# The MLP's down projection as seven products of half blocks, with the weights' sums made by accumulating DMAs

## The chip, the core and the metric

The kernel runs on one core of one Trainium2 chip, in one launch. A core has a matrix engine (TensorE, PE in the profile, with PEld for its weight loads), a vector engine (VectorE, DVE), a scalar engine (ScalarE, ACT), a general one (GpSimd, POOL), an engine that only issues DMAs (SyncE, SP), and 16 DMA engines. Each engine has a queue of its own and works it off in order; semaphores connect them. The metric is the device time of one execution in microseconds, the median of several runs.

## The reference

Two groups of 256 tokens go through one encoder layer with shared weights. The change concerns only its end, the MLP, where `x` has 512 rows (both groups), 1024 columns, and the hidden layer has 4096:

```python
h2 = rms_norm(x, norm2_g)
x = x + jnp.square(jax.nn.relu(h2 @ w_up)) @ w_down
...
return rms_norm(x, final_norm_g)
```

All of it is fp32. The norm's factor per token is taken out of the up projection: `relu(r*z)**2` is `r**2 * relu(z)**2`, so the factor is applied when the down projection's result is added.

## The kernel before

**Precision.** An fp32 product is made of three matmuls with operands in a faster format: each operand is split into a high part (ACT copies it with rounding) and a low part (DVE, in the attention part POOL, subtracts the high part from the original). `mm3` issues high x high, high x low, low x high. A "split" below means such a pair of instructions, "hi" and "lo" its two results.

**Weights.** A weight chunk is 128 x 1024 (512 KB). `chunk` has SP load it into one of two `raw` tiles and splits it into two of ten `w` tiles. `run` walks a list of units, each a function with the chunks that it needs; after a unit has been issued, the chunks of the next ones are fetched, three chunks ahead in the MLP (`ahead`), four in its last quarter. So in the queues of ACT and DVE the split of a chunk stands three units ahead of the unit that uses it. ACT, DVE and PE keep the order in which the program was written (`InOrder`); the DMAs of SP and GpSimd's instructions are placed by the framework, by when their tiles come free.

**The MLP.** `up` makes one tile of 128 hidden units for all 512 tokens: 24 matmuls of 128 x 512 (8 blocks of the inner dimension by three), then `r` = relu (ACT), its square (DVE), and the split of the square into `u` (ACT and DVE). There are four quarters of eight such tiles. After each quarter the down projection uses its eight tiles: for each half `hh` of the 1024 output columns and each block `t` of 128 tokens, 24 matmuls into one PSUM bank, then one DVE instruction (`add_down`) that adds the bank, times the token's factor `rr`, into `acc[t, hh]` in SBUF. Those start out as `x` turned back to rows of tokens (`turn_x1`, four PE transposes, a copy and a square on ACT).

**The end.** The last half of the last quarter is `last_down`: tokens block by block, so that the final norm of one block (`final`: a sum, a power on GpSimd, scaling on ACT and DVE, two DMAs out) runs beside the matmuls of the next.

Of the kernel before, what the change touches and what calls it, by code (L numbers as in the profile page):

```python
# [10 lines left out]
F32 = mybir.dt.float32  # L11
# [5 lines left out]
P = 128  # L17
# [60 lines left out]
def encoder_kernel(ctx: ExitStack, tc: tile.TileContext, a: dict, out: bass.AP):  # L78
# [4 lines left out]
    sb = ctx.enter_context(tc.tile_pool(name="sb", bufs=1))  # L83
    ps = ctx.enter_context(tc.tile_pool(name="ps", bufs=8, space=bass.MemoryType.PSUM))
    dr = ctx.enter_context(tc.tile_pool(name="dr", bufs=1, space=bass.MemoryType.DRAM))

    cnt = [0]

# [79 lines left out]
    def run():  # L168
        need = [(i, s) for i, (_, srcs) in enumerate(units) for s in srcs]
        got, at = [[] for _ in units], 0  # L170
        done = 0
        for i, (fn, srcs) in enumerate(units):
            done += len(srcs)
            for fetch in (True, False):
                while at < min(len(need), done + (0 if fetch else ahead[0])):
                    u, s = need[at]
                    got[u].append(chunk(*s))
                    at += 1
                if fetch:
                    fn(*got[i])  # L180

    def mm3(o, wh, wl, xh, xl, first, last):
        E.matmul(o, wh, xh, start=first, stop=False)
        E.matmul(o, wh, xl, start=False, stop=False)
        E.matmul(o, wl, xh, start=False, stop=last)

    def fm(w, X, o):

# [515 lines left out]
    def put_v12(t, p):  # L704

        b, i = divmod(t, 2)
        for rl in range(2):
            v = sb.tile([P, S], F32, tag="v12", name=nm("v12"), bufs=8)
# [105 lines left out]
        unit(out_proj, (a["w_o"][ff],))  # L814


    acc = {}
    ss = const("ss", [P, NT, 2])
    rr = const("rr", [P, NT])

    def turn_x1(t, hh):
# [25 lines left out]

    gf = []
    fs = const("fs", [P, NT, 3])
    fr = const("fr", [P, NT])  # L850

    def load_gf():
        for hh in range(2):
            g = wide("gf")
            A.dma_start(g, bass.AP(tensor=a["gf"].tensor, offset=a["gf"].offset + hh * T, ap=[[0, P], [1, T]]))
            gf.append(g)

    def add_down(t, hh, p, last=False):
        y = acc[t, hh]
        V.scalar_tensor_tensor(y, p, rr[:, t:t + 1], y, op0=ALU.mult, op1=ALU.add)  # L860
        if last:
            A.activation(wide("junk"), y, AF.Square, accum_out=fs[:, t, 0:1])
            V.tensor_tensor(y, y, gf[hh], op=ALU.mult)

    def final(t, c, n):

        r = fr[:, t:t + 1]
        V.tensor_reduce(r, fs[:, t, :n], axis=AX.X, op=ALU.add)
        V.tensor_scalar(r, r, 1.0 / D, EPS, op0=ALU.mult, op1=ALU.add)
        G.tensor_tensor(r, r, mhalf[:, 0:1], op=ALU.pow)  # L870
        V.tensor_tensor(acc[t, 1][:, c], acc[t, 1][:, c], gf[1][:, c], op=ALU.mult)
        A.activation(acc[t, 0], acc[t, 0], AF.Copy, scale=r)
        V.tensor_scalar(acc[t, 1], acc[t, 1], r, None, op0=ALU.mult)
        for hh in range(2):
            (A, SP)[hh].dma_start(out[t * P:(t + 1) * P, hh * 512:(hh + 1) * 512], acc[t, hh])

    def last_down(*ws):

        flush(NT)
        Uq = U[3]  # L880
        for t in range(NT):
            c = slice(t * P, (t + 1) * P)
            cols = ((0, 512),) if t < NT - 1 else ((0, 256), (256, 512))
            for part, (n0, n1) in enumerate(cols):
                p = bank()[:, :n1 - n0]
                for k in range(KD):
                    wh, wl = ws[k // 2]
                    w = slice((k % 2) * 512 + n0, (k % 2) * 512 + n1)
                    mm3(p, Uq[k][:, 0, c], Uq[k][:, 1, c], wh[:, w], wl[:, w], k == 0, k == KD - 1)
                y = acc[t, 1][:, n0:n1]  # L890
                V.scalar_tensor_tensor(y, p, rr[:, t:t + 1], y, op0=ALU.mult, op1=ALU.add)
                A.activation(wide("junk")[:, n0:n1], y, AF.Square, accum_out=fs[:, t, 1 + part:2 + part])
                if n1 < 512:
                    V.tensor_tensor(y, y, gf[1][:, n0:n1], op=ALU.mult)
            final(t, slice(n0, n1), 1 + len(cols))

    for qq in range(4):
        for ff in range(KD):
            unit(lambda w, qq=qq, ff=ff: up(w, qq, ff), (a["w_up"][8 * qq + ff],))
            if qq == 0:  # L900
                unit(lambda ff=ff: turn_x1(ff // 2, ff % 2))
        if qq == 0:
            unit(inv_ms)
            unit(load_gf)
        uq = U.setdefault(qq, [])
        if qq == 3:
            unit(lambda: ahead.__setitem__(0, 4))
        for hh in range(2):
            srcs = [a["w_dn"][qq, hh, i] for i in range(4)]
            if qq == 3 and hh:  # L910
                unit(last_down, *[(s,) for s in srcs])
            else:
                def after(t, p, hh=hh, qq=qq):
                    if qq < 3:
                        add_down(t, hh, p)
                    else:
                        later.append(lambda: add_down(t, hh, p, True))

                for u in tm(uq, srcs, 512, after):
                    unit(*u)  # L920
    run()


# [72 lines left out]
```

## Time and profile before

| what | us |
|---|---|
| median of 3 runs (871.85 to 873.25) | 871.92 |
| the profiled execution, its own time | 871.41 |
| its span, first to last instruction | 869.6 |
| PE busy in it | 858.7 |
| DVE busy | 390.1 |
| ACT busy | 344.7 |
| POOL busy | 192.6 |
| DMA: mean rate over the span | 101 GB/s |

The page's first part gives the busy time of each engine; the second cuts the span into 40 slices with the busy tenths; the fourth follows the chain of work that ended last; the fifth groups instructions by line and operation. Most instructions have line 72, since a helper records them, so groups are told by their tiles' names. In an answer of the timeline a row is: start, duration, engine, line, operation, output<-inputs, shape, count, and in brackets how long the engine had been idle and what ended that. A duration there reaches a little into the next row, since an engine starts an instruction before the one ahead has quite finished.

### The profile page before, as it was taken

The page shows a single profiled execution, that of the slowest core. Times are in us where ns is not written, and L with a number is a line of the kernel's source. Part 1 is how long each engine was busy: PE and PEld are TensorE (multiplying, and loading weights), DVE is VectorE, ACT ScalarE, POOL GpSimd, SP SyncE. Part 2 cuts the span into 40 slices and gives each one's busy share as a digit, 9 for nine tenths or more (in the row PEclk, how much of TensorE's full clock was granted, in tenths as well). Part 3 has the DMA queues.
Part 4 walks back from the last instruction along what each step waited for, and adds up shares of the span by engine and source line. Part 5 has one row for each costly group of instructions (what it writes and reads, how often), then busy time and mean ns, then how long its engine had stood idle before and what let it go on. Part 6 is the DMA issues. An engine that isn't in the chain of part 4 may idle for free.

```text
span 869.6 us, 10683 instructions
## 1 busy us (share of the span) xinstructions
PE 858.7 (99%) x4176; PEld 717.3 (82%) x4176; DVE 390.1 (45%) x625; ACT 344.7 (40%) x606; POOL 192.6 (22%) x133
## 2 busy tenths in 40 slices
PE   9999999999999999999999999999999999999997
PEld 8778998888888888888887888888888888888886
DVE  6595445456443213333436444433453345334543
ACT  6364555565654332232224335521342144214432
POOL 2315455547556551112212000000000000000001
PEclk9999999999999999999999999999999999999999
DMA  8342223233332122222323432332223222322222
GB/s 284 113 136 88 83 73 103 80 93 98 106 94 71 51 87 96 96 86 97 121 73 99 149 117 96 122 119 74 95 98 121 74 95 98 123 73 93 97 77 98
DMA packets 41851, 88.00 MB, mean 101 GB/s; under 512 B 18734, under 2 KB 18980, under 8 KB 41800
## 3 DMA queue, kind: packets, MB, share of 16 engines
q1 hardware_dynamic: 39272, 83.07, 29.3%
q10 hardware_dynamic: 2304, 4.20, 1.5%
q8 instruction: 33, 0.54, 0.3%
q14 instruction: 18, 0.15, 0.1%
q0 software_dynamic: 224, 0.05, 0.0%
HBM read 85.15 MB, written 2.14 MB: 100 GB/s over the span
## 4 chain that ended last, share of the span: by engine, by line
PE 88%; DVE 4%; ACT 2%; DMA 2%; issue 2%; POOL 1%; SPq 0%; POOLq 0%; DVEq 0%; ACTq 0%
PE ps L72 81%; PE sc L72 3%; PE o L72 2%; PE tp L72 2%; DMA mr<-in_memT 1%; DMA raw<-in_w_mem 1%; ACT sp L72 1%; DVE sp L72 1%; DVE w L72 1%; DVE mg L72 0%; ACT w L72 0%; DVE st L72 0%; DVE qq L72 0%; DVE kl L72 0%; DVE sq L72 0%
## 5 line engine op out<-in xcount | busy, mean ns | idle before, releaser
L72 PE MATMUL ps<-x,w 128*128 128x512 f32 x1080 | 252.4, 391 | 0.0
L72 PEld LDWEIGHTS ps<-x,w 128*128 128x128 f32 x1080 | 200.8, 188 | 41.5
L72 DVE TENSOR_TENSOR w<-raw,w 128x1024 fp32r<-128x1024 f32 (+1 forms) x107 | 131.3, 1234 | 128.7 <-ACT w L72 128.6
L72 ACT ACTIVATE w<-raw 128x1024 fp32r<-128x1024 f32 (+2 forms) x144 | 149.1, 1040 | 95.4 <-DMA raw<-in_w_dn 37.4
L72 PE MATMUL ps<-h,w 128*128 128x512 f32 x768 | 176.7, 390 | 0.0
L72 PE MATMUL ps<-w,u 128*128 128x512 f32 (+1 forms) x792 | 175.1, 383 | 0.0
L72 PEld LDWEIGHTS ps<-w,u 128*128 128x128 f32 x792 | 145.5, 188 | 29.0
L72 PEld LDWEIGHTS ps<-h,w 128*128 128x128 f32 x768 | 143.6, 188 | 29.6
L158 POOL TENSOR_TENSOR w<-raw,w 128x1024 fp32r<-128x1024 f32 (+1 forms) x37 | 87.3, 2361 | 117.8 <-ACT w L72 95.0
L870 POOL TENSOR_TENSOR fr<-fr,mhalf 128x1 f32<-128x1 f32 x4 | 3.5, 870 | 395.9 <-DVE fr L72 395.9
L72 ACT ACTIVATE r<-ps 128x512 f32<-128x512 f32 x32 | 19.1, 598 | 114.4 <-PE ps L72 114.4
L72 DVE TENSOR_TENSOR r<-r 128x512 f32<-128x512 f32 x32 | 22.1, 692 | 70.8 <-ACT r L72 70.8
L72 ACT ACTIVATE sp<-sp,st 128x256 f32<-128x256 f32 (+1 forms) x48 | 25.8, 538 | 57.7 <-DVE st L72 57.7
L72 DVE SCALAR_TENSOR_TENSOR acc<-ps,rr,acc 128x512 f32<-128x512 f32 (+1 forms) x33 | 24.2, 733 | 54.3 <-PE ps L72 54.3
L72 PE MATMUL ps<-mg,w 128*128 128x512 f32 x192 | 44.3, 390 | 1.5 <-ACT mg L72 0.9
L72 ACT ACTIVATE g<-ps 128x512 f32<-128x512 f32 x16 | 9.6, 598 | 91.0 <-PE ps L72 91.0
L72 PEld LDWEIGHTS ps<-mg,w 128*128 128x128 f32 x192 | 36.0, 188 | 9.6 <-ACT mg L72 1.3
L72 PE MATMUL ps<-w,x 128*128 128x384 f32 (+1 forms) x192 | 39.9, 363 | 0.0
L72 DVE TENSOR_TENSOR sum<-o,lo 64x256 f32<-64x256 f32 x24 | 10.0, 418 | 66.5 <-ACT lo L72 66.4
L457 POOL TENSOR_TENSOR sp<-sp,st 128x512 f32<-128x512 f32 (+1 forms) x32 | 36.7, 1147 | 6.5 <-DVE st L72 3.6
L72 PEld LDWEIGHTS ps<-w,x 128*128 128x128 f32 x192 | 34.3, 188 | 3.6
L72 DVE TENSOR_TENSOR u<-r,u 128x512 fp32r<-128x512 f32 x32 | 22.2, 692 | 22.4 <-ACT u L72 22.4
(135 smaller groups left out, 814.4 us busy)
## 6 DMA issues: line engine op xcount, KB each, us to landing
raw<-in_w_up SPq DMA_DIRECT2D x32, 512.0 KB, 3.2
raw<-in_w_dn SPq DMA_DIRECT2D x32, 512.0 KB, 3.3
raw<-in_w_g SPq DMA_DIRECT2D x24, 512.0 KB, 3.3
raw<-in_w_b SPq DMA_DIRECT2D x12, 512.0 KB, 3.2
raw<-in_w_bam SPq DMA_DIRECT2D x8, 512.0 KB, 3.2
raw<-in_w_o SPq DMA_DIRECT2D x8, 512.0 KB, 3.3
raw<-in_w_mem SPq DMA_DIRECT2D x7, 512.0 KB, 4.3
bias<-scr SPq DMA_DIRECT2D x48, 64.0 KB, 3.0
```

The source lines that it names most:

```text
L72: return self.tc.keep_in_program_order(method(*args, **kw))
L158: sub[0].tensor_tensor(lo[:, c], raw[:, c], f(hi[:, c]), op=ALU.subtract)
L457: G.tensor_tensor(s[:, :, :w], s[:, :, :w], st[:, 6:8].unsqueeze(2).to_broadcast([P, 2, w]), op=ALU.mult)
L870: G.tensor_tensor(r, r, mhalf[:, 0:1], op=ALU.pow)
```

## The change

The down projection's inner dimension is now taken in eight pieces `c` of 512 (four tiles of `up`). Within a piece both matrices are cut into 2 x 2 halves: A11, A12, A21, A22 (tokens by hidden units, 256 x 256) and B11, B12, B21, B22 (hidden units by output columns, 256 x 512). Instead of eight products of halves, seven are made of sums and differences of halves (`product`), each of 12 matmuls of 128 x 512 for two blocks of 128 tokens, in four pairs of PSUM banks, a, c, d and e. P1 and P2 share bank a, Q5 and Q3 bank d, P7 and Q4 bank e: the second adds onto what the first has left there, after DVE has read the first.

What the seven products need and leave:

- the weights' halves and their sums. A piece has four `blk` tiles (`load_blocks`, SP's DMAs). The tile T is B11 at first; after each split DVE and ACT are through with it, and a DMA issued by GpSimd with `accum_op=ALU.add` adds the next half from DRAM onto it: P1 uses B11, Q5 the sum with B12, Q6 that with B22, Q4 that with B21. C is B12 with B22 added in the same way.
- the sums of A (`form`): up to one DVE subtraction each, then a split (ACT copy, DVE subtraction).
- the sums of the products (`add_to`): each bank is added by DVE into one of five accumulators (V, G, 11, 12, 21; two tiles each), the first time copied by ACT. The final combination with the residual is made once, in the last piece (`last_sums`).

`up` now takes the square on ACT, in fp32, without a split. The units are put in turn: in a piece, a product of the piece before stands between two tiles of `up`, four of the seven so, and three more follow without a tile of `up` between them. After the last tile of `up` ten products are left: P7, Q3, Q4 of piece 6 and all seven of piece 7, the latter in the order P1, Q5, P2, Q6, P7, Q3, Q4. The residual goes to DRAM (`x1d`) and comes back before the last piece. The pools of the attention (`at`) are closed before the MLP so that `blk` has room.

The diff, cut to its core:

```diff
+    def load_blocks(c):
+
+        if c in blocks:
+            return
+        t = {n: block_tile() for n in "T2BC"}
+        for n, b in (("T", "11"), ("2", "21"), ("C", "12"), ("B", "22")):
+            SP.dma_start(t[n], block(c, b))
+        G.dma_start(t["C"], block(c, "22"), accum_op=ALU.add)
+        blocks[c] = t
+
+    def parts(c, n):
+
+        def go():
+            load_blocks(c)
+            hi, lo = w_tile(), w_tile()
+            src = blocks[c][n[0]]
+            A.activation(hi, src, AF.Copy)
+            V.tensor_tensor(lo, src, f(hi), op=ALU.subtract)
+            if n[1:]:
+                G.dma_start(src, block(c, n[1:]), accum_op=ALU.add)
+            return hi, lo
+        return go
...
+    PRODUCTS = dict(P1=("T12", "a", "V", -1), P2=("2", "a", "11", 1), Q5=("T22", "d", "G", 1),
+                    Q6=("T21", "c", "V", 1), P7=("C", "e", "G", -1), Q3=("B", "d", "12", 1), Q4=("T", "e", "21", 1))
+
+    def product(w, c, name):
+        _, bk, to, sign = PRODUCTS[name]
+        x = forms.pop((c, name))
+        new = name in ("P1", "Q5", "Q6", "P7")
+        for i in range(2):
+            if new:
+                banks[bk, i] = bank()
+            p = banks[bk, i]
+            for j in range(2):
+                t = slice(j * S + i * P, j * S + (i + 1) * P)
+                k = slice(j * 512, (j + 1) * 512)
+                mm3(p, x[:, 0, t], x[:, 1, t], w[0][:, k], w[1][:, k], new and j == 0, j == 1, not new)
+        flush(9)
+        ps_ = [banks[bk, i] for i in range(2)]
+        if c < NC - 1:
+            later.append(lambda: [add_to(to, i, ps_[i], ALU.add if sign > 0 else ALU.subtract) for i in range(2)])
+        else:
+            later.append(lambda: last_sums(name, ps_))
...
+            elif name == "Q6":
+                add_to("V", i, p)
+                for k in ("12", "G"):
+                    V.tensor_tensor(acc[k, i], acc[k, i], acc["V", i], op=ALU.add)
+                V.tensor_tensor(acc["21", i], acc["21", i], acc["V", i], op=ALU.subtract)
+                scaled(y[lo, 1], lo, 1, acc["12", i])
+                scaled(y[hi, 1], hi, 1, acc["G", i])
+                scaled(y[hi, 0], hi, 0, acc["21", i])
+            elif name == "P7":
+                finish(hi, 1, y[hi, 1], p, -1)
+            elif name == "Q3":
+                finish(lo, 1, y[lo, 1], p)
+                final(lo)
...
+    def finish(t, hh, y, p, sign=1):
+        scaled(y, t, hh, p, sign)
+        A.activation(h2("junk"), y, AF.Square, accum_out=fs[:, t, hh:hh + 1])
+        V.tensor_tensor(y, y, gf[0][:, hh], op=ALU.mult)
...
+    for c in range(NC):
+        for m in range(4):
+            if c:
+                down(c - 1, m)
+                make(c - 1, m + 3)
+            unit(lambda w, ff=4 * c + m: up(w, ff), (a["w_up"][4 * c + m],))
+            if c == 0:
+                unit(lambda m=m: turn_x1(m, 0))
+                unit(lambda m=m: turn_x1(m, 1))
...
+        for n in range(3):
+            if c:
+                down(c - 1, 4 + n)
+            make(c, n)
+    unit(fetch_x1)
+    for n in range(7):
+        down(NC - 1, n)
+        if n < 4:
+            make(NC - 1, n + 3)
+    unit(lambda: flush(9))
```

Three places show how the queues stand now. The first is ACT between the first MLP tiles and the first down product. Before, around the fourth tile of `up` (r is the relu, u the hi of the square, w a chunk's hi, acc and junk the transposed residual):

```order
L72 ACTIVATE r_4530<-ps_4505 128x512
L72 ACTIVATE u_4533<-r_4530 128x512
L72 ACTIVATE w_4537<-raw_4536 128x1024
L72 ACTIVATE acc_4547<-tp_4542 128x512
L72 ACTIVATE junk_4549,ss<-tp_4542 128x512
L72 ACTIVATE r_4576<-ps_4551 128x512
```

Now, from the relu of the fourth tile to the hi of P1's form (f_4604):

```order
L72 ACTIVATE r_4573<-ps_4548 128x512
L72 ACTIVATE u_4493<-r_4573 128x512
L72 ACTIVATE w_4576<-blk_4432 128x1024
L72 ACTIVATE xt_4585<-tp_4580 128x512
L72 ACTIVATE junk_4587,ss<-tp_4580 128x512
L72 DMA x1d<-xt_4585 128x512
L72 ACTIVATE xt_4595<-tp_4590 128x512
L72 ACTIVATE junk_4597,ss<-tp_4590 128x512
L72 DMA x1d<-xt_4595 128x512
L72 ACTIVATE f_4604<-u_4376 128x512
```

Where the next tile's matmuls followed, a product follows that needs f_4604, at the end of ten ACT rows.

The second place is ACT after the last tile of `up`. Before, chunk after chunk was split, each from a tile of its own:

```order
L72 ACTIVATE r_6386<-ps_6361 128x512
L72 ACTIVATE u_6389<-r_6386 128x512
L72 ACTIVATE w_6393<-raw_6392 128x1024
L72 ACTIVATE w_6399<-raw_6398 128x1024
L72 ACTIVATE w_6433<-raw_6432 128x1024
```

Now, from that tile's relu on (w_6742 is for Q4 of piece 6; w_6760, w_6782, w_6806 and w_6839 for P1, Q5, P2 and Q6 of piece 7; f are forms):

```order
L72 ACTIVATE r_6739<-ps_6712 128x512
L72 ACTIVATE u_6656<-r_6739 128x512
L72 ACTIVATE w_6742<-blk_6251 128x1024
L72 ACTIVATE w_6760<-blk_6564 128x1024
L72 ACTIVATE f_6765<-u_6528 128x512
L72 ACTIVATE w_6782<-blk_6564 128x1024
L72 ACTIVATE f_6789<-f_6787 128x512
L72 ACTIVATE w_6806<-blk_6565 128x1024
L72 ACTIVATE f_6810<-u_6656 128x512
L72 ACTIVATE w_6839<-blk_6564 128x1024
```

Three of the splits read the same tile, blk_6564 (T of piece 7): between each two of them lies an accumulating DMA that waits for the split ahead.

The third place is the end of DVE's queue. Before, four rows stood behind each of the last banks of matmuls (here the last block but one of tokens; fr is the norm's factor):

```order
L72 SCALAR_TENSOR_TENSOR acc_4639<-ps_6616,rr,acc_4639 128x512
L72 TENSOR_REDUCE fr<-fs 128x1
L72 TENSOR_SCALAR fr<-fr 128x1
L72 TENSOR_TENSOR acc_4639<-acc_4639,gf_4740 128x512
L72 TENSOR_SCALAR acc_4639<-acc_4639,fr 128x512
```

Now, from within the sums that follow Q6 (ps_6906 is its second bank) to P7's results (ps_6928 and ps_6935, the pair e, onto which Q4's matmuls add next):

```order
L72 SCALAR_TENSOR_TENSOR xt_6817<-acc_4798,rr,xt_6817 128x512
L72 SCALAR_TENSOR_TENSOR xt_6817<-acc_4948,rr,xt_6817 128x512
L72 TENSOR_TENSOR acc_4668<-acc_4668,ps_6906 128x512
L72 TENSOR_TENSOR acc_4923<-acc_4923,acc_4668 128x512
L72 TENSOR_TENSOR acc_4800<-acc_4800,acc_4668 128x512
L72 TENSOR_TENSOR acc_4950<-acc_4950,acc_4668 128x512
L72 SCALAR_TENSOR_TENSOR xt_6815<-acc_4923,rr,xt_6815 128x512
L72 SCALAR_TENSOR_TENSOR xt_6819<-acc_4800,rr,xt_6819 128x512
L72 SCALAR_TENSOR_TENSOR xt_6819<-acc_4950,rr,xt_6819 128x512
L72 SCALAR_TENSOR_TENSOR xt_6817<-ps_6928,nr,xt_6817 128x512
L72 TENSOR_TENSOR xt_6817<-xt_6817,gf_6821 128x512
L72 SCALAR_TENSOR_TENSOR xt_6819<-ps_6935,nr,xt_6819 128x512
```

Fourteen rows of sums stand between the forms of the last products and the row that frees P7's bank; behind them come the same five rows as before, four times.

More of the change, by code (lines that the diff above doesn't have):

```diff
@@ L176, in run @@
                     u, s = need[at]
-                    got[u].append(chunk(*s))
+                    got[u].append(s[0]() if callable(s[0]) else chunk(*s))
                     at += 1
@@ L180, in run, with mm3 @@
                     fn(*got[i])
[L182 to L185, printed above, removed]
+    def mm3(o, wh, wl, xh, xl, first, last, more=False):
+        E.matmul(o, wh, xh, start=first, stop=False, skip_group_check=more)
+        E.matmul(o, wh, xl, start=False, stop=False, skip_group_check=more)
+        E.matmul(o, wl, xh, start=False, stop=last, skip_group_check=more)
     def fm(w, X, o):
@@ L848, in encoder_kernel @@
[L848 to L863, printed above, removed]
@@ new lines, in encoder_kernel, with add_to @@
+    acc, banks = {}, {}
+    def add_to(k, i, p, op=ALU.add):
+        if (k, i) in acc:
+            V.tensor_tensor(acc[k, i], acc[k, i], p, op=op)
+        else:
+            acc[k, i] = h2("acc")
+            A.activation(acc[k, i], p, AF.Copy, scale=1.0 if op == ALU.add else -1.0)
+    PRODUCTS = dict(P1=("T12", "a", "V", -1), P2=("2", "a", "11", 1), Q5=("T22", "d", "G", 1),
+                    Q6=("T21", "c", "V", 1), P7=("C", "e", "G", -1), Q3=("B", "d", "12", 1), Q4=("T", "e", "21", 1))
@@ new lines, in encoder_kernel, with fetch_x1, scaled @@
+    xt, gf = {}, []
+    def fetch_x1():
+        for t in range(NT):
+            xt[t] = sb.tile([P, 2, 512], F32, tag="s4", name=nm("xt"), bufs=21)
+            SP.dma_start(xt[t], x1d[t].rearrange("p (h n) -> p h n", h=2))
+        g = sb.tile([P, 2, 512], F32, tag="s4", name=nm("gf"), bufs=21)
+        SP.dma_start(g, bass.AP(tensor=a["gf"].tensor, offset=a["gf"].offset, ap=[[0, P], [T, 2], [1, T]]))
+        gf.append(g)
+    def scaled(y, t, hh, src, sign=1):
+        V.scalar_tensor_tensor(y, src, (rr if sign > 0 else nr)[:, t:t + 1], y, op0=ALU.mult, op1=ALU.add)
@@ new lines, in last_sums @@
+    def last_sums(name, ps_):
+        for i in range(2):
+            p, lo, hi = ps_[i], i, i + 2
+            y = {(t, hh): xt[t][:, hh] for t in (lo, hi) for hh in range(2)}
+            if name == "P1":
+                add_to("V", i, p, ALU.subtract)
+            elif name == "Q5":
+                add_to("G", i, p)
+                scaled(y[lo, 0], lo, 0, acc["11", i])
+            elif name == "P2":
+                finish(lo, 0, y[lo, 0], p)
+            elif name == "Q6":
+                add_to("V", i, p)
[5 more added lines that the diff above has]
+                scaled(y[hi, 0], hi, 0, acc["21", i])
+            elif name == "P7":
+                finish(hi, 1, y[hi, 1], p, -1)
+            elif name == "Q3":
+                finish(lo, 1, y[lo, 1], p)
+                final(lo)
+            else:
+                finish(hi, 0, y[hi, 0], p)
+                final(hi)
@@ L872, in final @@
-        A.activation(acc[t, 0], acc[t, 0], AF.Copy, scale=r)
-        V.tensor_scalar(acc[t, 1], acc[t, 1], r, None, op0=ALU.mult)
+        A.activation(xt[t][:, 0], xt[t][:, 0], AF.Copy, scale=r)
+        V.tensor_scalar(xt[t][:, 1], xt[t][:, 1], r, None, op0=ALU.mult)
         for hh in range(2):
[L875 to L902, printed above, removed]
-            unit(inv_ms)
[L904 to L920, printed above, removed]
+            (A, SP)[hh].dma_start(out[t * P:(t + 1) * P, hh * 512:(hh + 1) * 512], xt[t][:, hh])
```

87 lines of the change are left out of this document (68 added, 19 removed).

## The prediction, made before the changed kernel ran

> **What bounds the kernel now.** First the page's engine table, then the chain of waits over the MLP, then the groups.
>
> ```profile
> span 869.6 us, 10683 instructions
> PE 858.7 (99%) x4176; PEld 717.3 (82%) x4176; DVE 390.1 (45%) x625; ACT 344.7 (40%) x606; POOL 192.6 (22%) x133
> 557.90 0.44 PE tp L72 x4
> 558.33 299.24 PE ps L72 x1320
> ```
>
> PE is busy 99% of the span, and from 558.33 on the chain is one run of 1320 matmuls: 299.24 / 1320 = 0.2267 us each. Nothing else ends last there, so a matmul less is worth 0.2267 us as long as PE stays fed. DVE has 55% to spare over the whole, which says nothing about one stretch.
>
> ```profile
> 863.34 0.48 DVE L72 SCALAR_TENSOR_TENSOR acc<-ps,rr,acc 128x256 f32<-128x256 f32 x1 [0.72 <-PE ps L72]
> 865.52 0.48 DVE L72 TENSOR_SCALAR acc<-acc,fr 128x512 f32<-128x512 f32 x1 [0.44 <-POOL fr L870]
> ```
>
> At the end PE is through at about 863.3; DVE's last row ends at 866.0, and the last DMA closes the span 3.6 us later. So 6.3 us lie behind PE now.
>
> **The change, part by part.**
>
> *Matmuls.* The down projection had 768 full-width matmuls (some as two halves); now 8 x 7 x 12 = 672. 96 x 0.2267 = **21.8 us** less on PE. This is the whole gain.
>
> *What the vector side costs.* The durations that I use:
>
> ```profile
> L72 DVE TENSOR_TENSOR w<-raw,w 128x1024 fp32r<-128x1024 f32 x68 | 82.7, 1224 | 45.4 <-ACT w L72 45.4
> L72 DVE TENSOR_TENSOR u<-r,u 128x512 fp32r<-128x512 f32 x32 | 22.2, 692 | 22.4 <-ACT u L72 22.4
> L72 DVE TENSOR_TENSOR xr<-ps,xr 128x512 f32<-128x512 f32 x8 | 5.5, 692 | 13.3 <-PE ps L72 12.1 <-DMA xr<-in_xT 1.2
> L72 DVE SCALAR_TENSOR_TENSOR acc<-ps,rr,acc 128x512 f32<-128x512 f32 x31 | 23.2, 750 | 53.5 <-PE ps L72 53.5
> L72 ACT ACTIVATE w<-raw 128x1024 fp32r<-128x1024 f32 x138 | 144.5, 1051 | 93.9 <-DMA raw<-in_w_dn 37.4 <-DMA raw<-in_w_up 20.4 <-PE ps L72 19.3
> L72 ACT ACTIVATE u<-r 128x512 fp32r<-128x512 f32 x32 | 20.2, 633 | 24.3 <-DVE r L72 24.3
> 580.15 0.75 DVE L72 SCALAR_TENSOR_TENSOR acc<-ps,rr,acc 128x512 f32<-128x512 f32 x1 [0.61 <-PE ps L72]
> 580.82 2.35 DVE L72 TENSOR_TENSOR w<-raw,w 128x1024 fp32r<-128x1024 f32 x2
> 467.21 1.28 DVE L72 TENSOR_TENSOR g<-ps,g 128x512 f32<-128x512 f32 x2
> ```
>
> Rows without a wait between them overlap: 0.67 us from an add with scale (0.75) to the next row, 2.35 - 1.23 = 1.12 from one weight split to the next, 1.28 - 0.69 = 0.59 (taken as 0.60) for a 128x512 row. A piece asks of DVE 11 weight splits, 11 rows for forms and 14 sums: 11 x 1.12 + 25 x 0.60 = 27.3 us, beside 180 matmuls = 40.8 us on PE. So over a whole piece DVE's work is hidden, and ACT's too (11 x 1.05 + 15 x 0.63 = 21 us). Three places are not hidden.
>
> *Seam after the fourth tile (once).* P1's form stands behind ten ACT rows. In the trace, from one such relu on:
>
> ```profile
> 522.23 0.60 PE L72 MATMUL tp<-ident,xr 128*128 128x128 f32 x4
> 522.49 0.60 ACT L72 ACTIVATE r<-ps 128x512 f32<-128x512 f32 x1 [1.97 <-PE ps L72]
> 524.38 1.04 ACT L72 ACTIVATE w<-raw 128x1024 fp32r<-128x1024 f32 x1
> 525.33 0.58 ACT L72 ACTIVATE acc<-tp 128x512 f32<-128x512 f32 x1
> 525.81 0.59 ACT L72 ACTIVATE junk<-tp 128x512 f32<-128x512 f32 x1
> 526.29 0.20 ACT L72 ACTIVATION_READ_ACCUMULATOR junk<-tp 128x1 f32 x1
> 470.45 0.34 ACTq L72 DMA_DIRECT2D xr<-in_xT  x1
> ```
>
> The relu starts 0.26 after PE has gone on from its tile; relu and square 0.53 each (0.63 less the overlap), the split 0.95, twice (copy 0.48, square 0.48, read-out 0.20, store 0.34), then the form 0.63: 0.26 + 1.06 + 0.95 + 3.0 + 0.63 = 5.9 us, while PE has two groups of transposes, 0.88. PE stands **5.0 us**.
>
> *Seams of pieces 1 to 6 (six times).* From E, the end of a piece's fourth tile, PE does P7, Q3 and Q4 (2.72 us each), then P1, a tile (5.44), P2. ACT does relu, square, Q4's hi until E+2.5. DVE then does Q4's lo (to 3.8), P1's lo (4.9), its form (5.5), P7's first sum (6.1). Q4's matmuls add onto P7's bank and wait for that: 6.15 instead of 5.44, 0.7 us. DVE goes on with a sum, lo, form, two sums, lo, Q5's two form rows with ACT between (0.73), two sums, lo, Q6's form likewise, and then P1's first sum: 6.0 + 0.6 + 1.1 + 0.6 + 1.2 + 1.1 + 1.9 + 1.2 + 1.1 + 1.9 + 0.7 = 17.5, with latencies 17.7, and P2 wants P1's bank at 17.0: 0.7 us. Together 6 x 1.4 = **8.4 us**; bounds are 0 and, if rows didn't overlap (20 rows x 0.08 more), 3 us a seam.
>
> *The accumulating DMAs.* The trace has none of this size. Nearest rows:
>
> ```profile
> raw<-in_w_dn SPq DMA_DIRECT2D x32, 512.0 KB, 3.3
> scr<-tb POOLq DMA_DIRECT2D x6, 6.0 KB, 1.9
> mr<-in_memT SPq DMA_DIRECT2D x8, 256.0 KB, 5.8
> ```
>
> A plain load of 512 KB lands after 3.3 us, one from GpSimd of almost nothing after 1.9; the bytes make 1.4. The accumulate must fetch the old value too: 1.9 + 2 x 1.4 = 4.7, with issue and other traffic I take **6 us**. Ends: 3.3 (as the plain one), and 11.6 (twice the slowest, 5.8). [...] Within a piece Q5's lo ends 3.6 us behind one tile, and Q6's split is wanted on PE 12.7 us later, less 2.3 for the split: 10.4 us are free, so 6 costs nothing there.
>
> [...]
>
> *The last ten products.* PE's work behind the last tile's end E is 10 x 2.72 = 27.2 us. DVE's queue there, counted from Q4's lo (piece 6): 8 weight splits; 37 128x512 rows (11 of forms, 10 sums of earlier products, 8 of Q6's, 8 multiplications by the gain); 16 with scale; four finals. 8 x 1.12 + 37 x 0.60 + 16 x 0.67 = 41.9. A final's rows in the trace:
>
> ```profile
> 852.15 0.75 DVE L72 SCALAR_TENSOR_TENSOR acc<-ps,rr,acc 128x512 f32<-128x512 f32 x1 [1.01 <-PE ps L72]
> 852.94 0.63 ACT L72 ACTIVATE junk<-acc 128x512 f32<-128x512 f32 x1 [1.56 <-DVE acc L72]
> 853.69 0.16 DVE L72 TENSOR_REDUCE fr<-fs 128x1 f32<-128x2 f32 x1 [0.79 <-ACT junk L72]
> 854.12 0.94 POOL L870 TENSOR_TENSOR fr<-fr,mhalf 128x1 f32<-128x1 f32 x1 [3.50 <-DVE fr L72]
> 855.10 0.49 DVE L72 TENSOR_SCALAR acc<-acc,fr 128x512 f32<-128x512 f32 x1 [0.46 <-POOL fr L870]
> ```
>
> small rows 0.66 each, 2.6 for four: **44.5 us** of DVE. It starts at E+2.6. Its waits, in order: P1's lo ends at 5.0, the accumulate lands at 11.0, Q5's hi ends at 12.1, DVE being idle from 6.7: 5.4. The next accumulate costs 1.1. Four forms with ACT in the middle, 0.73 each: 2.9. P2's and P7's results, whose multiplication waits for ACT's square: 4 x 0.73 = 2.9. Four finals that in addition wait for GpSimd's power: 4 x 2.0 = 7.9, in series, since each stands ahead of the next in the queue. Q4's split behind two squares on ACT, and rows that use the row ahead: 1.5. 2.6 + 44.5 + 21.7 = 68.8: DVE ends at **E+69**, the span at E+72.6. PE meanwhile waits: Q4 (piece 7) needs P7's bank, which DVE reads only behind Q6's 14 sums.
>
> *E.* 863.3, less the 96 saved and the 120 that come behind E (216 x 0.2267 = 49.0), plus 5.0 + 8.4: 827.7. **Sum:** 827.7 + 72.6 = 900.3; the profiled execution's time was 871.41 - 869.6 = 1.8 above its span, and 0.5 below the median: **902 us**, slower by 30. That is -21.8 + 5.0 + 8.4 and 39 behind PE's work, where 6.3 were.
>
> The 8 early `blk` loads (SP, at the attention's end) and the two accumulates I cost at nothing: chunks are split three units (16 us) ahead.
>
> **Rivals.**
>
> *DVE's rest hides beside PE* (faster). If sums and finals drained beside the last products and only 6.3 us remained behind PE, with the first seam alone paid: 871.4 - 21.8 + 5.0 = 855. For it speaks DVE's 55% idle time. The point from which it decides: DVE's end must come before E + 27.2 + 6.3 + (21.8 - 13.4) - 3.6 = E+38. DVE's rows alone, without a wait, take 44.5. So 6%.
>
> *Slow accumulates.* At 11.6 us Q6's split comes too late in every piece: 1.2 us (11.6 - 10.4) on PE, and since DVE falls back with that split, an estimated 1.7 more at the next seam, 6 x 2.9 = 17; and the tail's chain has two of them in series, 2 x 5.6 = 11: 930. For it: none was ever seen at this size, and the loads from SP share the DMA engines. 15%.
>
> *About even* (within 0.2%, what a measurement of this kernel can tell from no change): only by the losses adding up to 21.8 by chance. 3%.
>
> **How the numbers follow.** The forecast, 902, has 76%. Without seams at 1.4, without the first, and with 3.3 for an accumulate it would be 885; with seams of 3 us and 10 us for an accumulate, 920. The range, 884 to 925, takes in part of the slow accumulates. Faster 6%, same 3%, slower 91%.
>
> **What would show it.** PE's matmuls fall by about 120 instructions, its busy share below 96%; its digit in the last two or three slices falls to about half while DVE's stands at 7 to 9; the chain's last 50 us are DVE, ACT and POOL rows. Q4's first matmuls of pieces 1 to 6 wait for DVE under 1 us. An accumulate's time to landing is under 10 us. Wrong would be: waits of PE on `w` hi in every piece (slow accumulates), or a tail under 40 us behind the last tile of `up`.

## The result, and the profile after

| | before | after |
|---|---|---|
| median of the runs, us | 871.91 (871.85 to 873.25) | 902.31 (901.70 to 903.09) |
| span of the profiled execution | 869.6 | 900.3 |
| PE busy | 858.7 | 850.9 |
| DVE busy | 390.1 | 475.2 |

The changed kernel takes 1.0345 times as long, 95% interval 1.0327 to 1.0363: 30.4 us slower. The forecast was 902.

First the page of the changed kernel: the engines' busy times, and from the 40 slices (22.5 us each) the rows of PE, DVE and PE's granted clock.

```profile
span 900.3 us, 10765 instructions
PE 850.9 (95%) x4056; PEld 704.4 (78%) x4056; DVE 475.2 (53%) x756; ACT 402.3 (45%) x694; POOL 218.4 (24%) x165
PE   9999999999999999999999989999999999999642
DVE  6594444565533204334354424656675766575684
PEclk9999999999999999999999998999999999999885
```

PE has 120 instructions less. But for one 8, where the first seam lies, it stays at 9 until the last three slices, where it falls to 6, 4 and 2; DVE has 6, 8 and 4 there, and the granted clock 8, 8 and 5. So the work saved is there, and most of the time is lost at the end. Who PE waits for is in the view of its waits (waited for, us in total, times, longest):

```profile
PE ps L72 <- DVE xt L72: 12.4, 1, 12.4
PE ps L72 <- DVE acc L72: 11.0, 13, 5.1
PE ps L72 <- ACT f L72: 6.4, 2, 4.1
```

Of the 13 waits for `acc` one is long (5.1); the other twelve are 5.9 us together, seven at Q4 (0.55 each) and five at P2 (0.41 to 0.45): the first piece's seam has only the one at Q4. The 4.1 is the seam after the fourth tile. The 12.4 is Q4 of the last piece. The timeline from the last tile of `up` on, the rows that carry the argument:

```profile
829.56 5.60 PE L72 MATMUL ps<-w,f 128*128 128x512 f32 x24
834.66 0.86 POOL L895 DMA_DIRECT2D blk<-in_w_dn  x1 [14.01 <-DVE w L72]
840.07 1.06 ACT L72 ACTIVATE w<-blk 128x1024 fp32r<-128x1024 f32 x1 [6.63 <-DMA blk<-in_w_dn]
841.16 1.23 DVE L72 TENSOR_TENSOR w<-blk,w 128x1024 fp32r<-128x1024 f32 x1 [5.00 <-ACT w L72]
...
853.23 12.99 PE L72 MATMUL ps<-w,f 128*128 128x512 f32 x48 [5.05 <-DVE acc L72]
...
868.75 0.68 DVE L72 TENSOR_TENSOR acc<-acc,ps 128x512 f32<-128x512 f32 x1
869.47 1.90 DVE L72 TENSOR_TENSOR acc<-acc,acc 128x512 f32<-128x512 f32 x3
871.28 2.07 DVE L72 SCALAR_TENSOR_TENSOR xt<-acc,rr,xt 128x512 f32<-128x512 f32 x3
...
877.78 0.74 DVE L72 SCALAR_TENSOR_TENSOR xt<-ps,nr,xt 128x512 f32<-128x512 f32 x1
878.67 5.46 PE L72 MATMUL ps<-w,f 128*128 128x512 f32 x12 [12.45 <-DVE xt L72]
...
895.91 0.49 DVE L72 TENSOR_SCALAR xt<-xt,fr 128x512 f32<-128x512 f32 x1 [0.66 <-POOL fr L1010]
```

E, the end of the last tile of `up`, is 829.56, where P7 begins. An accumulating DMA is issued at 834.66, and ACT can split its tile at 840.07, 5.4 us later. From 868.75 DVE works through Q6's fourteen sums without a pause; only then comes the row that reads P7's bank (877.78), and 0.9 us later PE's last product starts. DVE's last row ends at 896.4, E + 66.8.

The same stretch by engine (columns: stretch, its length, busy us and instructions of PE, PEld, DVE, ACT, POOL, granted clock, DMA share, GB/s):

```profile
870.00:877.00 7.00, 0.00 (x0) 0.00 (x0) 6.96 (x12) 0.00 (x0) 0.00 (x0) 0.56 0.00 0
877.00:884.00 7.00, 5.33 (x12) 3.80 (x12) 4.63 (x8) 2.17 (x6) 0.00 (x0) 0.50 0.00 0
```

In the first of these only DVE works. In the second PE is back, at a granted clock of 0.50.

Last the DMAs of the MLP, from the page's sixth part (KB each, median us from issue to landing):

```profile
blk<-in_w_dn POOLq DMA_DIRECT2D x32, 512.0 KB, 5.8
raw<-in_w_up SPq DMA_DIRECT2D x32, 512.0 KB, 5.8
```

The accumulates land after 5.8 us. The plain loads of `up`'s weights beside them need 5.8 where they needed 3.2 before.

### The profile page after: what moved, and what is told of

Same layout as the page of the kernel before. It is cut to its first block, busy times and chain, and to the rows that moved or that the text cites. A ratio compares the mean times of both kernels' runs of the same rounds, so it can differ in the third digit from the quotient of the medians.

```text
span 900.3 us, 10765 instructions
## 1 busy us (share of the span) xinstructions
PE 850.9 (95%) x4056; PEld 704.4 (78%) x4056; DVE 475.2 (53%) x756; ACT 402.3 (45%) x694; POOL 218.4 (24%) x165
## 3 DMA queue, kind: packets, MB, share of 16 engines
q0 software_dynamic: 4832, 16.83, 11.2%
## 4 chain that ended last, share of the span: by engine, by line
PE 74%; DVE 14%; ACT 6%; issue 4%; DMA 1%; POOL 0%; POOLq 0%; DVEq 0%; SPq 0%; ACTq 0%
PE ps L72 67%; DVE w L72 4%; DVE acc L72 3%; PE sc L72 2%; PE o L72 2%; DVE f L72 2%; PE tp L72 2%; DVE xt L72 2%; ACT w L72 2%; ACT f L72 1%; DMA blk<-in_w_dn 1%; ACT sp L72 1%; DVE sp L72 1%; ACT r L72 1%; ACT junk L72 1%
## 5 line engine op out<-in xcount | busy, mean ns | idle before, releaser
L72 PE MATMUL ps<-w,f 128*128 128x512 f32 x672 | 168.6, 406 | 29.9 <-DVE xt L72 12.4
L72 PEld LDWEIGHTS ps<-w,f 128*128 128x128 f32 x672 | 130.3, 196 | 63.6 <-issue 17.9
L72 PE MATMUL ps<-h,w 128*128 128x512 f32 x768 | 179.7, 390 | 0.0
L72 PEld LDWEIGHTS ps<-h,w 128*128 128x128 f32 x768 | 144.1, 188 | 29.9
L72 DVE TENSOR_TENSOR w<-raw,w 128x1024 fp32r<-128x1024 f32 (+1 forms) x75 | 92.4, 1236 | 94.9 <-ACT w L72 94.8
L72 ACT ACTIVATE w<-raw 128x1024 fp32r<-128x1024 f32 (+2 forms) x112 | 115.6, 1035 | 20.8 <-DMA raw<-in_w_mem 7.2
L72 DVE TENSOR_TENSOR w<-blk,w 128x1024 fp32r<-128x1024 f32 x56 | 67.3, 1223 | 102.5 <-ACT w L72 102.5
L895 POOL DMA_DIRECT2D blk<-in_w_dn x24 | 20.8, 866 | 281.1 <-DVE w L72 281.1
L72 ACT ACTIVATE w<-blk 128x1024 fp32r<-128x1024 f32 x56 | 57.2, 1045 | 12.5 <-DMA blk<-in_w_dn 9.3
L72 DVE TENSOR_TENSOR acc<-acc,ps 128x512 f32<-128x512 f32 x94 | 60.2, 680 | 0.0
L72 ACT ACTIVATE f<-f 128x512 fp32r<-128x512 f32 x32 | 20.2, 632 | 86.7 <-DVE f L72 86.7
```

The source lines that it names most:

```text
L72: return self.tc.keep_in_program_order(method(*args, **kw))
L895: G.dma_start(src, block(c, n[1:]), accum_op=ALU.add)
```

## The experiments

The theory: the loss is DVE's queue behind the last tile of `up`, worked off in order, with small losses at the seams. The rivals: the accumulating DMAs, through their latency or their traffic; PE's wait for P7's bank; PE's lower clock. Four kernels leave one thing out of the changed kernel each; the later ones look for a form that keeps the gain. Ratios are to the kernel before, in runs on the same chip.

### No accumulating DMAs

```diff
-        G.dma_start(t["C"], block(c, "22"), accum_op=ALU.add)
...
-            if n[1:]:
-                G.dma_start(src, block(c, n[1:]), accum_op=ALU.add)
```

> All the accumulating DMAs are left out, so the weights' sums are not made: three tiles are split unsummed, and the rest runs as in the changed kernel. Theory (the loss is DVE's queue behind the last tile of up): only the chain of T's splits behind that tile gets shorter, by the 5.0 us that DVE stands before the second split and about 1 us at the third, so 896 us (894 to 898); the pieces still take 42.3 us each. Rival (the accumulates and their traffic are the loss): the pieces fall to about 41 us and the tail by 10 or more, 875 to 885 us.

Measured: 895.72 us (ratio 1.0262, 1.0245 to 1.0278). PE in its timeline, from E on:

```profile
829.10 5.60 PE L72 MATMUL ps<-w,f 128*128 128x512 f32 x24
835.25 8.41 PE L72 MATMUL ps<-w,f 128*128 128x512 f32 x36 [0.55 <-DVE acc L72]
846.82 12.48 PE L72 MATMUL ps<-w,f 128*128 128x512 f32 x48 [3.16 <-DVE acc L72]
872.25 5.20 PE L72 MATMUL ps<-w,f 128*128 128x512 f32 x12 [12.95 <-DVE xt L72]
```

E moves by 0.5 us and what follows it by 6. So over the pieces the accumulates cost next to nothing that PE sees, though the loads of `up` land in 3.2 us again here; the tail keeps its 12.9 us wait. The rival falls as the main cause: without any accumulate 24 of the 30 us are still lost.

### Plain loads in their place

```diff
-        G.dma_start(t["C"], block(c, "22"), accum_op=ALU.add)
+        G.dma_start(t["C"], block(c, "22"))
...
-                G.dma_start(src, block(c, n[1:]), accum_op=ALU.add)
+                G.dma_start(src, block(c, n[1:]))
```

> The same DMAs of GpSimd without the addition: they overwrite the tile, so the weights' sums are left out, but the waits stay. Theory: a plain load lands 1 to 2 us sooner than the 5.4 of an accumulate, and the chain behind the last tile of up holds two of them, of which the second is nearly hidden: 900 to 901 us. Rival (the addition itself, with its second read, is the loss): near what the kernel without these DMAs gives, under 890 us.

Measured: 899.74 us (1.0314, 1.0296 to 1.0331). The transfers land after

```profile
blk<-in_w_dn POOLq DMA_DIRECT2D x32, 512.0 KB, 3.7
```

So the addition makes 2.1 us of the 5.8, and 2.6 us of the whole time, a little more than was expected. In the page's table of queues the same 16.83 MB take 11.2% of the 16 DMA engines' span with the addition and 5.7% without: the addition about doubles the engines' time.

### Lighter sums behind Q6

```diff
             elif name == "Q6":
                 add_to("V", i, p)
-                for k in ("12", "G"):
-                    V.tensor_tensor(acc[k, i], acc[k, i], acc["V", i], op=ALU.add)
-                V.tensor_tensor(acc["21", i], acc["21", i], acc["V", i], op=ALU.subtract)
-                scaled(y[lo, 1], lo, 1, acc["12", i])
-                scaled(y[hi, 1], hi, 1, acc["G", i])
-                scaled(y[hi, 0], hi, 0, acc["21", i])
```

> Of the 14 rows of DVE behind Q6 in the last piece 12 are left out (six combinations of 0.60 us, six additions to the residual of 0.67), so most sums miss in the output. Theory: DVE is the bound there, so the span falls by the rows' 7.6 us: 894.7 us (893 to 896). Rival (PE at half clock, or ACT, GpSimd and the finals' latencies are the bound): less than 2 us, 900 to 902 us.

Measured: 894.16 us (1.0248, 1.0227 to 1.0270), 8.1 us less than the changed kernel. The twelve rows had been counted at 7.6 us. In the profiled executions E to the span's end is 62.7 us (830.49 to 893.2) instead of 70.7, so 8.0 less. The time falls by about what DVE no longer does, and the rival's less than 2 us is out.

### A bank of its own for Q4

```diff
-        new = name in ("P1", "Q5", "Q6", "P7")
+        new = name in ("P1", "Q5", "Q6", "P7") or (c == NC - 1 and name == "Q4")
```

> In the last piece Q4 gets a pair of banks of its own instead of adding onto P7's, so that its first matmul no longer waits 12.4 us for DVE; P7's part of two of the output's four quarters is left out. DVE has the same rows in the same order. Theory: DVE's queue is the bound, PE's wait is only its shadow: 902 us (901 to 903), with Q4's matmuls some 12 us earlier. Rival (PE's wait is what the change lost at the end): 12 us faster, 890 us.

Measured: 901.18 us (1.0329, 1.0311 to 1.0346). PE's last product and DVE's last row:

```profile
866.94 3.16 PE L72 MATMUL ps<-w,f 128*128 128x512 f32 x11 [0.24 <-DVE w L72]
894.55 0.49 DVE L72 TENSOR_SCALAR xt<-xt,fr 128x512 f32<-128x512 f32 x1 [0.66 <-POOL fr L1010]
```

PE is through at 870.1, 14 us earlier than in the changed kernel (878.67 + 5.46 = 884.1), and the time is 1.1 us shorter. Even that is not the bank's: in this execution E itself came 1.2 us earlier (828.38), since the 12 matmuls behind the first seam took 4.26 us there instead of 5.32 (see the last section), and from E to DVE's last row it is 66.7 us instead of 66.8. So the longest wait of PE in the changed kernel cost next to nothing: it was DVE's backlog seen from PE. PE's lower clock in its last product is answered with it: that product ended at 884.1 at a granted clock of 0.50, and with PE through 14 us sooner the end does not move. P1's product of the last piece, slowed to 4.47 us in the changed kernel (granted clock 0.64), took 3.29 here (1.00), and that did not move it either. At the first seam the clock does cost time, as the next kernel shows.

### P1's first form earlier

```diff
+            if c == 0 and m == 2:
+                make(0, 0)
...
-            make(c, n)
+            if c or n:
+                make(c, n)
```

> P1's form of the first piece is issued two tiles of transposes earlier, behind the third tile of up; nothing else is changed. Theory: PE's wait of 4.1 us at the first product goes and the rest shifts: 898.2 us (897.5 to 899). Rival (what is gained there stands at the next product, whose split or form is then late): 901 to 902 us.

Measured: 899.00 us (1.0299, 1.0282 to 1.0316), 3.3 us less: at the upper end of the theory's 897.5 to 899 (its runs go from 896.7 to 900.7). The wait at the first product goes, but at the second PE now waits 2.0 us. P2 adds onto P1's bank, which the first time is copied by ACT, and that copy stands in ACT's queue behind two forms for which ACT waits for DVE. How much was lost at each place shows in PE's timeline, first of the changed kernel, then of this one:

```profile
541.05 5.53 PE L72 MATMUL ps<-w,f 128*128 128x512 f32 x12 [4.07 <-ACT f L72]
546.37 5.70 PE L72 MATMUL ps<-h,w 128*128 128x512 f32 x24
```

```profile
548.25 4.61 PE L72 MATMUL ps<-w,f 128*128 128x512 f32 x12 [2.00 <-ACT acc L72]
552.69 3.57 PE L72 MATMUL ps<-h,w 128*128 128x512 f32 x15
```

The 12 matmuls behind the wait took 5.32 us (541.05 to 546.37) instead of 2.72, so 4.07 + 2.6 = 6.7 us were lost; here they took 4.44, so 2.0 + 1.7 = 3.7. The difference, 3.0, is near the 3.3 by which the medians differ.

### The last piece as plain products

The seven-product form stays in pieces 0 to 6. In piece 7 `up` splits its tiles as the kernel before did, and the sums of the pieces are added to the residual as they come. P1's early form from the run above is in this kernel and in all that follow, though the lines below do not show it:

```diff
+        if c == NC - 1:
+            V.tensor_tensor(r, r, r, op=ALU.mult)
+            u = s4("u")
+            two(r, u[:, 0], u[:, 1])
+            U.append(u)
+            return
...
+    def last_down(*ws):
+        ws = (ws[:2], ws[2:])
+        for t in range(NT):
+            c = slice(t * P, (t + 1) * P)
+            for hh in range(2):
...
+    unit(last_down, *[(a["w_dn"][3, hh, i],) for hh in range(2) for i in (2, 3)])
```

> Pieces 0 to 6 stay seven products; the last piece is eight products of halves in the order of token blocks (96 matmuls instead of 84), as at the end of the kernel before, with the sums of the seven products added to the residual beside these matmuls, and with the early form. Nothing is left out. Theory: the tail behind PE's last matmul is again the 6.3 us of the kernel before, 84 matmuls less are 19.0 us, the pieces lose 1.5 us each (42.3 against 40.8) and some 2 us stand elsewhere: 871.4 - 19.0 + 6 x 1.5 + 2 = 863 us (860 to 868), faster than both. Rival (the sums of seven products cost as much wherever they stand, the tail only moves): 875 or more.

Measured: 874.47 us (1.0026, 1.0015 to 1.0037). 28 of the 30 us come back; the early form alone gave 3.3 of them, so some 24.5 are the last piece's. But 863 was expected: a miss of 11, and only half a us from the rival's 875. One block of tokens on DVE in its timeline:

```profile
854.38 0.69 DVE L72 TENSOR_TENSOR blk<-blk,gf 128x512 f32<-128x512 f32 x1 [0.79 <-ACT junk L72]
...
856.52 0.16 DVE L72 TENSOR_REDUCE fr<-fs 128x1 f32<-128x2 f32 x1 [0.79 <-ACT junk L72]
...
857.92 0.49 DVE L72 TENSOR_SCALAR blk<-blk,fr 128x512 f32<-128x512 f32 x1 [0.46 <-POOL fr L1032]
...
859.86 0.69 DVE L72 TENSOR_TENSOR blk<-blk,gf 128x512 f32<-128x512 f32 x1 [0.79 <-ACT junk L72]
```

A block comes round every 5.48 us (854.38 to 859.86), of which DVE waits 0.79 twice and 0.46 once, each time for a result that another engine is still making from DVE's own. PE gives a block every 5.44. So DVE never makes up the lag with which it enters, and PE's last matmul ends 11 us ahead of the span's end instead of 6.3. PE also waits 0.8, 2.7 and 0.9 us behind the last tile of `up`, where DVE does splits and sums in one queue. "Beside the matmuls" had been taken for granted: the queue's length was counted, not its waits.

### Forms behind the tile

```diff
             if c:
                 down(c - 1, m)
-                make(c - 1, m + 3)
             unit(lambda w, ff=4 * c + m: up(w, ff), (a["w_up"][4 * c + m],))
+            if c:
+                make(c - 1, m + 3)
...
-            if c or n:
-                make(c, n)
+            if c or n == 2:
+                for k in ((), (0,), (1, 2))[n] if c else (1, 2):
+                    make(c, k)
```

> As the kernel with the last piece plain, and in each piece the next forms are issued behind the tile of up instead of ahead of it, so that DVE reads P1's and P7's banks some 1.9 us earlier. Theory: the two waits of PE on an accumulator, about 0.5 us each in six pieces, go: 5 to 6 us less than the kernel with the last piece plain. Rival (the waits move to the forms or the splits): within 1 us of it.

Measured: 872.67 us (1.0001, 0.9991 to 1.0010), so 1.8 us less, not 5 to 6. Of the two waits in a piece the one at P2 is gone; the one at Q4, 0.55 us, stays, and behind the last tile PE waits 4.3 us where it was 2.7.

### Finals one block later

```diff
+                    if not hh and t:
+                        rest(t - 1)
...
+        rest(NT - 1)
...
+            raw, hi, lo = sb.tile([P, 1024], F32, tag="s4", name=nm("raw"), bufs=21), w_tile(), w_tile()
...
-            V.tensor_tensor(r, r, r, op=ALU.mult)
+            A.activation(r, r, AF.Square)
```

`rest` holds the last rows of `final`: the scaling on ACT and DVE and the DMAs out.

> As last_plain_seams, with three edits behind the last tile of up: each block's last scaling stands in DVE's and ACT's queues behind the first addition of the next block instead of ahead of it, the last two weight chunks have tiles of their own to land in, and the square of the last piece's tiles is made by ACT. Nothing is left out. Theory: DVE now gives 5.48 us to a block, as long as PE's 5.44, so the lag it starts with (2.9 us, and PE's waits of 4.3 and 1.0 us ahead of it) stays to the end; with the waits for ACT and GpSimd filled by the next block's rows a block takes about 4.1 us, the lag goes within three blocks, and some 4 us of the 872.7 go: 868 us (865 to 870). Rival (the latency of one block's norm is the bound, not the queue): within 1 us of 872.7.

Measured: 866.94 us (0.9942, 0.9928 to 0.9956): faster than the kernel before. The gain came, for another reason than given: a block still takes 5.45 us, since ACT's scaling of the block before now stands ahead of the square that DVE waits for. What went is PE's waiting ahead of the blocks (2.2 us instead of 4.3, and none of 1.0, 0.8 and 0.5); PE's last matmul still ends 10.9 us ahead of the span's end. Which of the three edits did it was not separated.

### GpSimd makes the low parts

```diff
     unit(mlp_pool)
+    unit(lambda: sub.__setitem__(0, G))
```

> As piped, and GpSimd instead of DVE makes the low parts of the chunks that are loaded plainly (32 for up, two of the last four; all four of the last piece), 2.36 us each where DVE took 1.14 in its queue. Theory: DVE's queue is what PE waits for at the seams and behind the last tile of up; with one to four splits less there the waits of PE (0.55 at each seam, 4.3 and 0.8 after the last tile) mostly go: 860 us (857 to 864), faster than the kernel before by over 0.9%. Rival (GpSimd's longer split, or its accumulating DMAs now queued behind splits, come too late): no faster than piped.

Measured: 867.02 us (0.9949, 0.9936 to 0.9963), the same as without: the rival's time. PE's waits of 0.55 us at the seams are all still there, and it waits 1.1 us for a split on GpSimd. DVE has 24 us less to do, and some of its rows became slower. From the groups by form, first of this kernel, then of the one without the edit (count, busy us, mean ns):

```profile
L72 DVE SCALAR_TENSOR_TENSOR blk<-acc,rr,blk 128x512 f32<-128x512 f32 x12 | 17.7, 1494 | 0.1
L72 DVE SCALAR_TENSOR_TENSOR blk<-ps,rr,blk 128x512 f32<-128x512 f32 x15 | 11.2, 745 | 0.2
```

```profile
L72 DVE SCALAR_TENSOR_TENSOR blk<-acc,rr,blk 128x512 f32<-128x512 f32 x12 | 8.7, 744 | 0.1
L72 DVE SCALAR_TENSOR_TENSOR blk<-ps,rr,blk 128x512 f32<-128x512 f32 x15 | 11.2, 745 | 0.2
```

Of these rows the ones with both tensors in SBUF double on average (the timeline has single ones of 2.2 us, as at 825.15 and 827.96, beside four splits on GpSimd from 824.14 to 835.2, and others of 0.75 where GpSimd is idle, as at 805.31); the ones that read one of the two from PSUM do not change. What makes those rows longer, beyond that they stand beside these splits, the runs do not show.

### Another order of the products

```diff
-    ORDER = ("P1", "P2", "Q5", "Q6", "P7", "Q3", "Q4")
+    ORDER = ("P1", "P7", "Q5", "Q6", "P2", "Q3", "Q4")
```

with the order of the finals' rows as in the next kernel.

> As piped, with two edits of order. The products of a piece run P1, P7, Q5, Q6, P2, Q3, Q4, so that every product that adds onto another's bank stands at least a tile of up behind it; behind the last tile of up only two rows of sums per product are left. In the last blocks ACT's square stands ahead of the last scaling of the block before, and DVE's multiplication by the gain behind the next addition. Nothing is left out. Theory: PE's waits for an accumulator (0.55 us and about 0.2 of restart, six times) and for Q4's bank (2.2, and 1.7 at a lower clock) go, and a block takes 4.2 us of DVE instead of 5.45, so that the lag is gone by the last block: 867 - 4.5 - 4 - 3 = 855.5 us (853 to 860), faster than the kernel before by 1.4 to 2.2%. Rival (P7's sums and the earlier accumulate only move the waits into T's splits, 8.2 us apart instead of 16): 864 or more.

Measured: 905.37 us (1.0372, 1.0353 to 1.0391): a miss of 50 us. The rival's time, 864 or more, came true, but not its mechanism: PE waits for no split.

```profile
PE ps L72 <- DVE acc L72: 35.6, 7, 6.1
665.10 7.68 PE L72 MATMUL ps<-h,w 128*128 128x512 f32 x24 [4.91 <-DVE acc L72]
```

The wait is no longer at a product but ahead of the fourth tile of `up` (`ps<-h,w`), which adds onto nothing and needs only a free bank. In this order P1's, P7's and Q5's pairs are all kept for their second product, and with Q6's pair all eight banks are taken; the tile waits until DVE has read Q6. The 24 matmuls behind it took 7.5 us instead of 5.44; the granted clock of the whole run is 0.970, where the kernel with the finals one block later has 0.991.

### The finals' order, then the order of products within the banks

Against the kernel with the finals one block later:

```diff
             elif name == "P7":
                 scaled(y[hi, 1], hi, 1, p, -1)
-                scaled(y[lo, 1], lo, 1, acc["V", i])
...
                 scaled(y[hi, 0], hi, 0, acc["V", i], -1)
+                scaled(y[lo, 1], lo, 1, acc["V", i])
...
-                    if hh and not part:
-                        V.tensor_tensor(xt[t][:, 0], xt[t][:, 0], gf[0][:, 0], op=ALU.mult)
                     V.scalar_tensor_tensor(y, p, rr[:, t:t + 1], y, op0=ALU.mult, op1=ALU.add)
+                    A.activation(h2("junk")[:, n0:n1], y, AF.Square, accum_out=fs[:, t, hh + part:hh + part + 1])
                     if not hh and t:
                         rest(t - 1)
-                    A.activation(h2("junk")[:, n0:n1], y, AF.Square, accum_out=fs[:, t, hh + part:hh + part + 1])
+                    if hh and not part:
+                        V.tensor_tensor(xt[t][:, 0], xt[t][:, 0], gf[0][:, 0], op=ALU.mult)
...
+        if c == NC - 1:
+            unit(lambda: ahead.__setitem__(0, 2))
```

> As piped, with the order of the products as there and two edits behind the last tile of up: in the last blocks ACT's square stands ahead of the last scaling of the block before and DVE's multiplication by the gain behind the next addition; and P7's two sums, on which Q4 waits, stand ahead of the split of the last piece's first chunk and of the additions of V. Nothing is left out. Theory: the lag of DVE, which stayed at about 4 us because a block took it 5.45 us, shrinks by about 1.2 in each of three blocks, and Q4's wait of 2.2 us halves: 867 - 3.6 - 1.5 = 862 us (860 to 864). Rival (one block's latency is the bound, or the rows moved behind are late instead): within 1 us of 867.

Measured: 861.35 us (0.9883, 0.9865 to 0.9901). Both edits did what they were to do: PE's wait for Q4's bank is 1.1 instead of 2.2, and at the last blocks DVE waits for PE again. To this, the order of products in pieces 0 to 5:

```diff
+    EARLY = ("P1", "P2", "Q5", "P7", "Q6", "Q3", "Q4")
...
-        name = ORDER[n]
+        name = (EARLY if c < NC - 2 else ORDER)[n]
```

> As order_a, and in pieces 0 to 5 P7 stands ahead of the fourth tile of up and Q6 behind it (P1, P2, Q5, P7, Q6, Q3, Q4). At most six of the eight banks are held then, where the order P1, P7, Q5, Q6, P2, Q3, Q4 held all eight when the fourth tile began. Nothing is left out. Theory (that order lost 4.9 us a piece for want of a free bank, not because of the accumulates): PE does not wait at the fourth tile, and the wait of 0.55 us with its restart of 0.2 at Q4 goes in six pieces: 4.5 us less than order_a. Rival (T's splits, two of which now stand 8.2 us apart, wait for their accumulates): PE waits on a weight's high part in each piece, and the time is that of order_a or more.

Measured: 856.19 us (0.9820, 0.9805 to 0.9835), 5.2 us less than the one above, where 4.5 was expected. Its page and PE's waits and rows:

```profile
span 854.2 us, 10773 instructions
PE 841.7 (99%) x4080; PEld 702.4 (82%) x4080; DVE 465.5 (55%) x742; ACT 397.6 (47%) x690; POOL 217.0 (25%) x161
...
PE ps L72 <- DVE blk L72: 0.9, 1, 0.9
PE ps L72 <- DVE w L72: 0.9, 1, 0.9
...
773.33 11.04 PE L72 MATMUL ps<-w,f 128*128 128x512 f32 x48
814.27 5.60 PE L72 MATMUL ps<-w,f 128*128 128x512 f32 x24
826.30 20.66 PE L72 MATMUL ps<-w,u 128*128 128x512 f32 x101 [0.92 <-DVE w L72]
```

The four products at a seam are one run of 48 matmuls without a wait. E is 814.3, which is what PE's work alone would give (863.3 less 19.0 for 84 matmuls and 29.9 for the 132 behind E: 814.4), and PE's last matmul ends 7.2 us ahead of the span's end. This kernel computes all that the reference asks for and beats the kernel before by 1.8%. It keeps 21 of the 24 accumulating DMAs that follow a split, as slow as they are (5.5 us).

## Why the prediction was right

*Matmuls, -21.8.* PE's instructions fell by the 120 named, and the change's E would be 814.3 without losses (863.3 - 21.8 - 27.2). Of the signs named, PE's digits came as forecast, DVE's (6, 8, 4) only in one slice.

*Seam after the fourth tile, 5.0.* 4.07 of waiting, and 2.6 more because the 12 matmuls behind it ran at a granted clock of 0.50: 6.7 in this execution. The clock was missing from the step.

*Seams of pieces, 1.4 each.* PE's rows of one piece, from P2 to the next P2:

```profile
678.05 2.98 PE L72 MATMUL ps<-w,f 128*128 128x512 f32 x12 [0.42 <-DVE acc L72]
...
702.63 5.60 PE L72 MATMUL ps<-w,f 128*128 128x512 f32 x24
708.78 5.69 PE L72 MATMUL ps<-w,f 128*128 128x512 f32 x24 [0.55 <-DVE acc L72]
...
720.36 2.97 PE L72 MATMUL ps<-w,f 128*128 128x512 f32 x12 [0.45 <-DVE acc L72]
```

A piece takes 42.3 us against 40.8 of matmuls: 1.5. Both places were the ones named, Q4 and P2, and both waits came down to some 0.5 us; about 0.25 more goes by around each (from 702.63 to 708.78 it is 6.15 us for 24 matmuls, where 5.44 is the least, and of the 0.7 only 0.55 shows as waiting). The edits that took away one cause each (forms behind the tile; P7 ahead of the tile) took away one wait each. The first of the six seams, at 582.54, has no wait at P2, so it cost 0.8; the prediction charged all six alike.

Together these make 6.7 + 0.8 + 5 x 1.5 = 15.0, and E came at 829.56, 15.3 behind PE's work; predicted were 13.4 and 827.7.

*Accumulating DMA, 6 us.* 5.8 by the page, 5.4 in the tail from issue to ACT's split. The doubled 1.4 us in the prediction's sum was an estimate: no run shows an accumulate fetch the old value, nor a transfer of twice the bytes. What the runs show is 5.8 against 3.7 us for the same transfer without the addition, and 11.2% against 5.7% of the DMA engines' time. The rival of slow accumulates had its deciding point at 10.4 us, and 5.8 stays well below.

*The last ten products.* E + 66.8 instead of E + 69. DVE's rows were 44.5 by the sum and are 46.5 in the trace's busy time; its waits were 21.7 and are 18: the first accumulate 5.0 instead of 5.4, and the finals 3.56 us apart instead of some 3.9, since GpSimd's power took 0.56 here instead of 0.94; the rest is in smaller waits. The 14 sums were named as what Q4 waits for, and the kernel with a bank of its own for Q4 shows that this wait was no loss of its own; the one with lighter sums, that the rows were. The rival that DVE's rest hides beside PE decided at E + 38, and DVE ended 29 us later.

*Sum.* 1.9 too early at E, 2.2 too late from there to DVE's last row: the mechanism held, but 902 against 902.3 is closer than its terms are, and that is luck. (The terms as written add up to 902.6.) The worst of them in proportion is the first seam, 5.0 for 6.7; in size it is DVE's waits, 21.7 for 18.

What the prediction did not say is how much of the loss can be had back. 28 of the 30 us came back with the last piece done plainly and P1's form made earlier, though that last piece saves no matmuls; the rest of the way to 856 was mostly the order of rows and products, at six seams and in four finals.

## What to carry to other kernels

An engine that is half idle over a kernel can still be the bound of its last 70 us: count its rows there, in queue order, with each wait for a result that goes through another engine and back. A saving that costs vector work pays where matmuls follow to cover it, so the last stretch is best left in the form with the least work behind the matmuls. An order of products that shares banks is checked against the number of banks, with the next tile's among them.

## What the hardware showed

*The granted clock after a wait.* The 5.32 us for 12 matmuls behind a wait of 4.07 were shown above; the granted clock was 0.50 over all of them. The slow stretch is not always as long: at the same place of the kernel in which Q4 has its own bank, behind 4.06 us, they took 4.26 (the next tile starts at 545.22), and the clock was 0.50 to 543.5 and 0.86 from there to 545.2.

```profile
540.96 4.42 PE L72 MATMUL ps<-w,f 128*128 128x512 f32 x12 [4.06 <-ACT f L72]
```

Shorter waits did it too, but not always. Behind 2.31 us 12 matmuls took 4.47 in the changed kernel, at a granted clock of 0.64 over them:

```profile
843.71 4.47 PE L72 MATMUL ps<-w,f 128*128 128x512 f32 x12 [2.31 <-ACT f L72]
```

Behind 2.23 us at the same place of the kernel in which Q4 has its own bank, by stretches:

```profile
842.40:845.70 3.30, 3.25 (x12) 2.10 (x12) 3.27 (x5) 1.46 (x2) 0.00 (x0) 1.00 0.85 137
```

The clock stayed at 1.00 (12 matmuls in 3.25 us of PE's time). Why the clock fell behind the one wait and not behind the other, the runs do not show. Around waits of 0.55 us 0.25 more went by, as shown at the seams.

*Plain loads beside accumulates.* The 512 KB loads of `up`'s weights took 5.8 us in the changed kernel, 4.1 with the same DMAs without the addition and 3.2 with none. The addition alone does not set it: in the last kernel, with accumulates of 5.5 us, these loads took 4.0. What else does is open. No run showed PE waiting for that.
